# Three drains ahead of the first group's first store in an RMSNorm-and-repeat kernel

## The chip, the cores and the metric

The kernel runs on one core of one Trainium2 chip. The metric is the device time of one execution in microseconds (us). The kernel before the change took 237.68 us, the median of 3 runs (237.47 to 237.84). One further execution was taken under the hardware profiler. It took 236.99 us, of which 235.7 us are the span of the profile, from the first profiled instruction of the program to the last.

## The reference

The input `x` has 8 x 512 = 4096 rows of 2048 float32 values. Each row is divided by its root mean square, multiplied by `gamma`, and written twice, one copy right behind the other. So 33.55 MB are read and 67.11 MB are written.

```python
B, S, D = 8, 512, 2048
x_rep = np.repeat(x, 2, axis=1)
rms = np.sqrt((x_rep ** 2).mean(axis=-1, keepdims=True) + 1e-6)
out = (x_rep / rms) * gamma[None, None, :]      # (8, 1024, 2048) float32
```

## The kernel before

**Tiles.** The 4096 rows are cut into four tiles of 1024 rows, numbered 0 to 3. In a tile each of the 128 partitions holds 8 neighbouring rows, 64 KB. One load (`load`, L50) brings a whole tile, 8.39 MB. A tile gives twice as many output rows, so it is stored in two halves, and each half is again 128 partitions x 64 KB (`store`, L56). There are 4 loads and 8 stores, all of one size, and all are issued by SyncE (SP) on one queue.

**The buffer.** One SBUF tensor `y` of 128 x 24 rows x 2048 holds everything. Its three regions are `first` (rows 0 to 7), `second` (8 to 15) and `third` (16 to 23). One tile of a group is loaded into rows 4 to 11, across `first` and `second`; the other is loaded into `third`.

**The steps.** `squares` (L69, L73, on ScalarE = ACT) makes sums of squares of some rows and their roots. `scale` (L82, L83, on VectorE = DVE) takes the reciprocal and multiplies each row by it and by `gamma`, into every second row of its target region. `repeat` (L90) copies those rows into the gaps between them; some of these copies run on ACT, some on DVE. Then `store` sends the region out.

**The order.** The order of the instructions on each engine is the order of the program (`manual_schedule`, no planner). The function `four` handles two tiles and is called twice, with tiles 0 and 1 (the first group) and with tiles 3 and 2 (the second group, `last=True`). In each call SP does, in this order: two loads, four stores. So its twelve transfers stand in one line: load, load, store x4, load, load, store x4. The loads of the second group go into space that stores of the first group read, so SP waits for those stores to land before it issues them.

**Around the change.** The first store of a group needs two copies: one on ACT and one on DVE. The latter is the return value `copied`. In the second group a helper `behind(copied)` puts 18 drains (`nc.sync.drain()`, L96) on SP ahead of that store. A drain here does nothing but occupy SP's instruction stream, and the first of the 18 waits for the copy on DVE. In the first group there is nothing of the kind: SP comes to the first store early and stands there in three waiting instructions (shown in the profile as EVENT_SEMAPHORE of L56) until the copy is done. These three wait for the five transfers of `gamma` and of tile 0 that have to have landed, and for DVE.

**The end.** After the last store ACT waits for the landing of the last but one store, spends time in three copies (L170), and SP waits for the landing of the last store (L173). This is not touched.

Of the kernel before, what the change touches and what calls it, by code (L numbers as in the profile page):

```python
# [9 lines left out]
def kernel(  # L10
# [38 lines left out]
    def load(n, at):  # L49
        nc.sync.dma_start(out=y[:, at : at + H * K, :], in_=x_t[n])  # L50
# [4 lines left out]
    def store(n, h, to, own=False):  # L55
        dma = nc.sync.dma_start(  # L56
            out=out_t[n, h], in_=y[:, to : to + K * R, :].rearrange("p j d -> p (j d)")
        )
        if own:
            tc.no_tile_sem_insts.add(dma.ins.name)  # L60
            dma.then_inc(landed[h], 16)

    def squares(at, rows):

        n = len(rows)
        ss = small.tile([P, n], f32, name=f"ss{n}")
        for c, k in enumerate(rows):
            sq = junk.tile([P, D], f32, name="sq")
            nc.scalar.activation(  # L69
                out=sq[:], in_=y[:, at + k, :], func=Act.Square, accum_out=ss[:, c : c + 1]  # L70
            )
        rms = small.tile([P, n], f32, name=f"rms{n}")
        nc.scalar.activation(out=rms[:], in_=ss[:], func=Act.Sqrt, scale=inv_d, bias=eps_t[:])  # L73
        return rms

    def scale(at, to, rows, rms, at_once=K):
        n = len(rows)
        rstd = small.tile([P, n], f32, name=f"rstd{n}")
        for c, k in enumerate(rows):
            if c % at_once == 0:  # L80
                part = slice(c, min(c + at_once, n))
                nc.vector.reciprocal(out=rstd[:, part], in_=rms[:, part])  # L82
            nc.vector.scalar_tensor_tensor(  # L83
                out=y[:, to + R * k, :], in0=y[:, at + k, :], scalar=rstd[:, c : c + 1],
                in1=gamma_b[:], op0=Alu.mult, op1=Alu.mult,
            )

    def repeat(to, k0, k1, copy):
        y_r = y[:, to + R * k0 : to + R * k1, :].rearrange("p (k r) d -> p k r d", r=R)
        return copy(out=y_r[:, :, 1, :], in_=y_r[:, :, 0, :]).ins  # L90

    STEPS = 18

    def behind(copied):
        for step in range(STEPS):
            drain = nc.sync.drain().ins  # L96
            if step == 0:
                tc.add_manual_dep(
                    drain, copied.name,
                    mybir.DependencyInfo(mybir.DependencyClass.Sync, mybir.DependencyReason.DATA),  # L100
                    reason="issue time",
                )
# [6 lines left out]
    def four(n, m, constants, at_once, last=False):  # L109


        load(n, first + K)
        constants()
        load(m, third)
        for rows, n_at_once in ((up[:half], half), (up[half:], at_once)):
            scale(first + K, first, rows, squares(first + K, rows), n_at_once)
        repeat(first, 0, half, nc.scalar.copy)
        copied = repeat(first, half, K, nc.vector.tensor_copy)
        if last:
            behind(copied)  # L120
        store(n, 0, first)
        scale(second, second, down, squares(second, down))
        repeat(second, half, K, nc.scalar.copy)
        repeat(second, 0, half, nc.vector.tensor_copy)
        store(n, 1, second)
        roots = [squares(third + h * K, up) for h in range(H)]
        scale(third, first, up, roots[0])
        repeat(first, 0, half, nc.scalar.copy)
        repeat(first, half, K, nc.scalar.copy)
        store(m, 0, first, last)  # L130
        scale(third + K, third, up, roots[1])
        repeat(third, 0, K, nc.scalar.copy)
        store(m, 1, third, last)
# [8 lines left out]
    def constants():  # L142
        nc.gpsimd.memset(eps_t, eps)  # L143

        nc.scalar.activation(out=gamma_s[0:1, 0, :1], in_=eps_t[0:1, :], func=Act.Sqrt)  # L145
        nc.scalar.dma_start(
            out=gamma_s[0:1, :, :C],
            in_=gamma[: G * C].rearrange("(p c d) -> p c d", p=1, c=G),
        )
        for c in range(E):  # L150
            at = G * C + c * G
            nc.scalar.dma_start(
                out=gamma_t[0:1, c * G : (c + 1) * G],
                in_=gamma[at : at + G].partition_broadcast(1),
            )
        nc.gpsimd.partition_broadcast(  # L156
            out_ap=gamma_b[:, : G * C].rearrange("p (c d) -> p c d", c=G),
            in_ap=gamma_s[0:1, :, :C],
        )
        nc.gpsimd.partition_broadcast(out_ap=gamma_b[:, G * C :], in_ap=gamma_t[0:1, : E * G])  # L160

    four(0, 1, constants, 1)
    four(3, 2, lambda: None, half, last=True)

    ctx.close()
# [38 lines left out]
```

## Time and profile before

| what | value |
|---|---|
| time, median of 3 runs | 237.68 us (237.47 to 237.84) |
| profiled execution: time, span | 236.99 us, 235.7 us |
| DVE busy | 84.4 us, 36% of the span |
| ACT busy | 127.6 us, 54% |
| SP's data queue (q1) | 1728 packets, 100.66 MB, 99.0% of 16 DMA engines |
| first store of the first group issued | 39.19 us |
| first store of the second group issued | 156.36 us |

Times are counted from the start of the span. The "share" of a DMA queue is the time that its packets took, summed and divided by 16 engines times the span: 99.0% says that the 16 DMA engines were almost never without a packet of this queue. A packet of the big transfers is one partition's 64 KB. Each transfer has 128 such packets, 8 for each of the 16 engines, so the page's 1728 packets are 12 transfers of 128 data packets and 16 small ones. In a table of windows a packet is counted whole in the window in which it starts; a share above 1 is therefore no error but says that packets that start in the window last beyond it.

### The profile page before, as it was taken

Reading aid. Unit: us, or ns where it says so; the run is one execution under the profiler, and the core shown is the slowest. Engines: PE = TensorE matmul, PEld = TensorE weight load, DVE = VectorE, ACT = ScalarE, POOL = GpSimd, SP = SyncE. Lnnn points to the kernel's source line nnn. Section 1 sums busy time; section 2 is a strip of 40 time slices with the busy share of each in tenths; the row PEclk is TensorE's granted clock in tenths of the full one; section 3 lists DMA queues with packets and bytes.
Section 4 is the critical chain, followed back from the end, with each engine's and each line's share of the span. In section 5 each row is a group of like instructions: output and inputs, shape, how many; then the busy total and the mean of one; then the engine's idle time right before and its main releaser. Section 6 shows DMA issues by size and latency. Waiting matters only on the chain. (4 is left out here: it accounts for less than half of the span.)

```text
span 235.7 us, 251 instructions
## 1 busy us (share of the span) xinstructions
DVE 84.4 (36%) x47; ACT 127.6 (54%) x89; POOL 2.9 (1%) x7
## 2 busy tenths in 40 slices
DVE  0000496594599500000000006938918993000000
ACT  2001989479999370000000049891999966502996
POOL 0110000000000000000000000000000000000000
DMA  9898989989898998989899898989889898989988
GB/s 356 357 534 356 523 367 389 501 356 534 356 523 368 467 423 367 523 356 534 356 456 434 356 534 356 534 356 523 367 389 501 356 534 356 534 356 489 400 356 357
DMA packets 1768, 100.69 MB, mean 427 GB/s; under 512 B 230, under 2 KB 230, under 8 KB 230
## 3 DMA queue, kind: packets, MB, share of 16 engines
q1 hardware_dynamic: 1728, 100.66, 99.0%
q10 hardware_dynamic: 38, 0.01, 0.0%
q14 instruction: 2, 0.02, 0.0%
HBM read 33.56 MB, written 67.11 MB: 427 GB/s over the span
## 5 line engine op out<-in xcount | busy, mean ns | idle before, releaser
L69 ACT ACTIVATE sq<-y 128x2048 f32<-128x2048 f32 x32 | 60.1, 1878 | 72.9 <-DMA y<-in_x_dram 72.2
L83 DVE SCALAR_TENSOR_TENSOR y<-y,rstd,gamma_b 128x2048 f32<-128x2048 f32 x32 | 73.8, 2348 | 1.8 <-DMA out_dram<-y 1.2
L90 ACT COPY y<-y 128x4096 f32<-128x4096 f32 (+1 forms) x10 | 42.6, 4283 | 19.2 <-DVE y L83 18.5
L82 DVE RECIPROCAL rstd<-rms 128x4 f32<-128x4 f32 (+2 forms) x11 | 1.8, 168 | 109.9 <-ACT rms L73 109.9
L170 ACT COPY y<-y 1x8192 f32<-1x8192 f32 (+1 forms) x3 | 17.4, 5876 | 13.0 <-ACTq L168 13.0
L90 DVE COPY y<-y 128x4096 f32<-128x4096 f32 x4 | 9.2, 2293 | 0.1
L69 ACT ACTIVATION_READ_ACCUMULATOR sq<-y 128x1 f32 x32 | 6.0, 186 | 0.0
L73 ACT ACTIVATE rms<-ss,eps_t 128x4 f32<-128x4 f32 (+1 forms) x10 | 3.0, 296 | 0.3
L156 POOL PARTITION_BROADCAST gamma_b<-y x1 | 2.2, 2245 | 9.8 <-DMA y<-in_gamma_dram 9.8
L145 ACT ACT_TABLE_LOAD x1 | 1.3, 1283 | 0.7 <-PEq L188 0.7
L160 POOL PARTITION_BROADCAST gamma_b<-y x1 | 0.3, 323 | 10.0 <-DMA y<-in_gamma_dram 10.0
L145 ACT ACTIVATE y<-eps_t 1x1 f32<-1x1 f32 x1 | 0.2, 202 | 0.0
L143 POOL MEMSET eps_t<- 128x1 f32 x1 | 0.1, 100 | 0.3 <-POOLq L188 0.3
L188 POOL MEMSET const-uint8-127<- 128x1 uint8 x1 | 0.1, 103 | 0.0
L188 POOL MEMSET const-float32-0.0<- 128x1 f32 x1 | 0.1, 99 | 0.2 <-issue 0.2
L188 POOL MEMSET const-bfloat16-1.0<- 128x1 bf16 x1 | 0.1, 101 | 0.0
L188 POOL MEMSET const-float32-1.0<- 128x1 f32 x1 | 0.1, 98 | 0.0
## 6 DMA issues: line engine op xcount, KB each, us to landing
out_dram<-y SPq DMA_DIRECT2D x8, 24.9
y<-in_x_dram SPq DMA_DIRECT2D x4, 31.4
y<-in_gamma_dram ACTq DMA_DIRECT2D x3, 0.1 KB
y<-in_gamma_dram ACTq DMA_DIRECT2D x1, 7.8 KB, 8.2
```

Of the source, the lines that this page charges most:

```text
L69: nc.scalar.activation(out=sq[:], in_=y[:, at + k, :], func=Act.Square, accum_out=ss[:, c : c + 1])
L73: nc.scalar.activation(out=rms[:], in_=ss[:], func=Act.Sqrt, scale=inv_d, bias=eps_t[:])
L82: nc.vector.reciprocal(out=rstd[:, part], in_=rms[:, part])
L83: nc.vector.scalar_tensor_tensor(out=y[:, to + R * k, :], in0=y[:, at + k, :], scalar=rstd[:, c : c + 1], in1=gamma_b[:], op0=Alu.mult, op ...
L90: return copy(out=y_r[:, :, 1, :], in_=y_r[:, :, 0, :]).ins
L143: nc.gpsimd.memset(eps_t, eps)
L145: nc.scalar.activation(out=gamma_s[0:1, 0, :1], in_=eps_t[0:1, :], func=Act.Sqrt)
L156: nc.gpsimd.partition_broadcast(out_ap=gamma_b[:, : G * C].rearrange("p (c d) -> p c d", c=G), in_ap=gamma_s[0:1, :, :C],)
L160: nc.gpsimd.partition_broadcast(out_ap=gamma_b[:, G * C :], in_ap=gamma_t[0:1, : E * G])
L170: done = nc.scalar.copy(out=y[0:1, a:b, :], in_=y[0:1, a:b, :])
L188: nc = _bacc.Bacc("TRN2", target_bir_lowering=False, num_devices=1)
```

## The change

`behind` takes the number of drains as an argument. It is now called in both groups: with 18 in the second, as before, and with 3 in the first. The first of the three drains waits for the DVE copy `copied`; the first store stands behind the third. In the built program SP's instructions ahead of that store are then, in order: drain (waits for DVE), drain, drain, the same three waiting instructions as before, the store. Nothing else is moved on any engine.

```diff
-    STEPS = 18
-
-    def behind(copied):
-        for step in range(STEPS):
+    def behind(copied, steps):
+        for step in range(steps):
             drain = nc.sync.drain().ins
             if step == 0:
                 tc.add_manual_dep(
...
         copied = repeat(first, half, K, nc.vector.tensor_copy)
-        if last:
-            behind(copied)
+        behind(copied, 18 if last else 3)
         store(n, 0, first)
```

## The prediction

> **What bounds the kernel now.** I read the page's busy times, its DMA queues and its chain first. DVE is busy for 36% of the span and ACT for 54%, while the queue that SP issues on fills 99.0% of the time of all 16 DMA engines. The chain of work that ended last names only the copies of L170, 7% of the span, which run beside the last store.
>
> ```profile
> span 235.7 us, 251 instructions
> ...
> DVE 84.4 (36%) x47; ACT 127.6 (54%) x89; POOL 2.9 (1%) x7
> ...
> q1 hardware_dynamic: 1728, 100.66, 99.0%
> ...
> ACT y L170 7%
> ```
>
> So the span is a line of packets. Each DMA engine carries 12 transfers x 8 packets = 96 packets of 64 KB. What one packet takes is read from the table of windows: in 154.90 to 155.50 us 1748 GB/s x 0.60 us = 1.049 MB started, 16 packets, and the share 4.03 x 0.60 us gives 2.418 us each. 96 x 2.418 = 232.1 us. The trace's records of single packets have the first packet at 1.73 us and the end of the last at 235.16 us, 233.4 us apart. All that is lost between the two is 1.3 us, and 0.9 of it is the very first row of packets (one took up to 3.30 us). Only two things can change the time: an engine that runs dry, or a packet that lasts longer than 2.418 us.
>
> The second view is the timeline around the two first stores, as lines of start, duration, engine, line and operation.
>
> ```profile
> 36.82 2.29 DVE L90 COPY y<-y 128x4096 f32<-128x4096 f32 x1
> ...
> 39.19 0.35 SPq L56 DMA_DIRECT2D out_dram<-y  x1
> ```
>
> ```profile
> 153.04 2.29 DVE L90 COPY y<-y 128x4096 f32<-128x4096 f32 x1
> ...
> 156.36 0.34 SPq L56 DMA_DIRECT2D out_dram<-y  x1
> ```
>
> In the first group the copy ends at 39.11 and the store is issued 0.08 us later. In the second it ends at 155.33 and the store comes 1.03 us later. What lies between them there is 18 drains and one waiting instruction.
>
> ```profile
> L96 SPq DRAIN  x18: 7/7/7, 155.4 to 156.2; - x18
> ```
>
> The third view is the table of windows (length, DVE, ACT, POOL, clock, DMA share, GB/s) around the seam between a group's second load and its first store, first group and then second.
>
> ```profile
> 38.60:39.20 0.60, 0.51 (x1) 0.60 (x1) 0.00 (x0) 1.00 4.08 1748
> 39.20:41.10 1.90, 0.00 (x0) 1.87 (x3) 0.00 (x0) 1.00 0.00 0
> ...
> 154.90:155.50 0.60, 0.43 (x1) 0.60 (x1) 0.00 (x0) 1.00 4.03 1748
> 155.50:157.30 1.80, 0.00 (x0) 1.77 (x3) 0.00 (x0) 1.00 0.00 0
> 157.30:157.90 0.60, 0.00 (x0) 0.57 (x3) 0.00 (x0) 1.00 4.05 1748
> ```
>
> The last row of 16 packets of the load starts in 38.60 to 39.20. No packet starts until 41.10, as every engine has one in hand; then the store's packets follow on. In the packet records the first engine to be free is so at 41.13 and the last at 41.76, and each goes on with the store in under 0.02 us. The reader is to see that the store was issued 41.13 - 39.19 = 1.94 us before anyone needed it.
>
> **The change part by part.** *The drains.* They delay nothing but SP. By the records of SP's instructions in the second group the drains stand 0.052 us apart (first at 155.363, last at 156.241, 17 steps), the waiting instruction follows 0.058 us behind the last, and the store 0.058 us behind that. Where SP has waiting instructions in a row (203.758, 203.820, 203.884, 203.946) they stand 0.063 us apart.
>
> *The three waiting instructions.* Before, SP had gone through two of them by 22.8 us and stood in the third, so they cost nothing after the copy. Now the first drain takes that wait, and all three come after it. Sum from the first drain (0.03 us behind the copy, as in the second group: 39.14): 2 x 0.052 + 0.058 + 2 x 0.063 + 0.058 = 0.35, so the store is issued at 39.49 and not 39.19. The delay is 0.30 us, twice what three drains alone are (0.16).
>
> *What it costs on the path.* The cover is the last row of the load, until 41.13. From 39.49 there are 1.64 us left. What a store needs from issue to its first packet the trace bounds but doesn't show: at the start of the program the first load was issued at 0.72 and its first packet began at 1.73, 1.01 us; in the second group the store was issued at 156.36, the first engine was free at 157.34, 0.98 us later, and went on at once. So 1.01 us is an upper bound from a cold queue and 0.98 from a running one. Both are under 1.64. I cost the delay at nothing; if the cover were gone, the whole 0.30 us would show.
>
> *Behind the store on SP* stand the waits of the second store, issued at 55.80, and of the third at 76.07; both wait for copies that end later than any of this. Nobody waits for this store's issue but DVE at L83, which waits 0.7 us for its landing (61.1), and the loads of the second group, issued at 100.10 and needed at 118.7. No DMA is added, none changes its place in the line, and no other engine's instructions move.
>
> *What it could gain.* The last row of the load differs in the two groups: 4.08 x 0.60 = 2.448 us a packet in the first, with the store issued 0.06 to 0.48 us after those packets started, and 4.03 x 0.60 = 2.418 in the second, issued 0.89 to 1.44 us after. That is 0.030 us x 16 = 0.48 us of lengthening in the first. By the packet records 0.215 of it falls on the engine that starts last and ends last (39.13 to 41.76), 0.10 and 0.08 on two others. With the change the store is issued 0.36 to 0.79 us after the starts, between the two cases. The gain is between 0 (the lengthening stays, or it is made up later: in the row that starts at 115.9 to 116.5 the other engines lose 0.1 to 0.44 us while this one loses 0.05) and 0.215 us (it goes, and nothing eats it). Whether the issue causes the lengthening no row tells. I take 0.08, nearer the low end, since by 118.7 us another engine is the last to finish and the lead of the others is spent.
>
> *Sum.* Span 235.66 - 0.08 + 0.00 = 235.58; the profiled execution 236.99 would be 236.91. The median of the runs shown lies 0.69 above the profiled one, and I leave that as it is: 237.68 - 0.08 = 237.6 us. A difference of 0.2%, 0.48 us, is about what a measurement of this kernel can tell from no change (its three runs lie 0.37 us apart).
>
> **A rule weighed here.** The row is the 0.98 us of the second group, with no idle DMA engine at the seam. The Trainium skill, page "DMA: Bandwidth & Descriptors", section "Rules for kernel authors", advises to issue a DMA early, because a fixed setup cost then overlaps with other work; its section on the anatomy of one DMA puts that fixed cost at about 2.0 us for the GpSimd path. Taken whole as a delay ahead of the first packet, that would be an estimate by that page of the Trainium skill of 39.49 + 2.0 = 41.49, a gap of 0.36 us at the seam, where the row gives none. By the same reckoning the second group's seam would have a gap of 1.0 us, and the trace shows none there, so I go by the row.
>
> **The rivals.** *The engines run dry at the seam (slower, but little).* If a store in the first group needed more than 1.64 us from issue to first packet, every engine would wait. For: the latency is not shown for this place. Against: 0.98 us sufficed at 156.36. A seam without idle time before caps the need at 1.94 us, so the gap is at most 1.94 - 1.64 = 0.30 us: 237.98 us, still within 0.2%.
>
> *The lengthening grows (slower).* The issue falls into the middle of the in-flight packets' first half and lengthens the last row more than now. For: rows exist that are far longer, 0.44 us at 116.0 where the line goes from store to load, and 0.88 us in the first row of all. Against: the later issue of the second group had none. With 0.88 on the engine that ends last in place of 0.215 the time is 237.68 + 0.67 = 238.35; with 0.44 it is 237.9. It decides from 0.69 us (0.215 + 0.48) on.
>
> *The lengthening goes, and more than one engine's share with it (faster).* If all 0.48 us of the row are carried one after another by the engine that sets the end, or the unprofiled runs, which are 0.69 us longer than the profiled one, lose more at this seam than the profiled one, the time is 237.68 - 0.48 = 237.2 or less. For: the second group with its later issue has a clean seam. Against: the records show 0.215 at most on one engine, and 0.30 us is only a third of the second group's delay.
>
> *It does nothing at all*, the last row is lengthened as before: 237.68, which the forecast cannot be told from.
>
> **How the numbers follow.** Forecast, with the case of no effect: 0.70. Running dry, up to 0.30 us: 0.06; both lie within 0.2%, so "same" has 0.76. Lengthening gone in a larger measure, over 0.48 us: 0.14, faster. Lengthening grown beyond 0.69 us: 0.10, slower. The range reaches from the faster rival's 237.2 to the dry seam's 237.98 and a little beyond, 238.05; it leaves out part of the two outer cases.
>
> **What would show it.** In the changed kernel's trace three drains of L94 stand at about 39.14 to 39.24, the first store is issued at 39.49 (39.34 if the three waiting instructions don't count), and the second group's store still 1.03 us behind its copy. In the windows the last row of load two starts in 38.6 to 39.2, the store's row from 41.1 on, and nothing lies idle between; the share of the first window tells whether the lengthening went (4.03) or stayed (4.08) or grew. The prediction is wrong if the store's first row starts later than 41.13 plus the longest packet, or if the queue's 99.0% falls, or if the time moves by more than 0.48 us while the seam looks the same.

## The result and the profile after

The changed kernel takes 238.40 us, the median of 20 runs, against 237.05 us for the kernel before, also of 20 runs. The first three of them are the runs with the median of 237.68 us that the prediction starts from; they lay high. The ratio is 1.0042, with a 95% interval of 1.0028 to 1.0056: 1.3 us slower, outside the range that was forecast.

The runs themselves say more than the median. Of the 20 runs of the changed kernel four lie at 236.9 to 237.0 us, where the kernel before has its fastest runs (from 236.84 on), and sixteen lie between 237.9 and 239.0 us. Of the kernel before only one run of the 20 was above 238.0 us, and 2 of 141 over all sessions. So the change does not add a constant to every execution. It makes a long kind of execution common that was rare. The profiled execution of the changed kernel (238.39 us, span 237.1 us) is of the long kind.

The page of the changed kernel, its queue and the row of the sums of squares (busy, mean, idle before and what ended it), and then the same row of the kernel before:

```profile
span 237.1 us, 254 instructions
...
q1 hardware_dynamic: 1728, 100.66, 98.6%
...
L69 ACT ACTIVATE sq<-y 128x2048 f32<-128x2048 f32 x32 | 60.1, 1878 | 74.5 <-DMA y<-in_x_dram 73.8
```

```profile
L69 ACT ACTIVATE sq<-y 128x2048 f32<-128x2048 f32 x32 | 60.1, 1878 | 72.9 <-DMA y<-in_x_dram 72.2
```

The queue's share fell from 99.0 to 98.6%, and ACT waits 1.6 us longer for tiles to land (73.8 us, before 72.2). The first store's copy and issue in the timeline of the changed kernel:

```profile
36.97 2.29 DVE L90 COPY y<-y 128x4096 f32<-128x4096 f32 x1
...
39.65 0.35 SPq L56 DMA_DIRECT2D out_dram<-y  x1
```

The copy ends at 39.26 and the store comes 0.39 us behind it; before it was 0.08. That is the change as it was meant, and nothing is late yet. The delay shows 100 us further on, where the second group begins. First the kernel before, then the changed one:

```profile
138.95 1.88 ACT L69 ACTIVATE sq<-y 128x2048 f32<-128x2048 f32 x1 [51.79 <-DMA y<-in_x_dram]
...
156.36 47.30 SPq L56 DMA_DIRECT2D out_dram<-y  x4
```

```profile
140.41 1.88 ACT L69 ACTIVATE sq<-y 128x2048 f32<-128x2048 f32 x1 [53.31 <-DMA y<-in_x_dram]
...
157.82 0.34 SPq L56 DMA_DIRECT2D out_dram<-y  x1
```

Tile 3 is there 1.46 us later, and the second group's first store is issued 1.46 us later. The loss has arisen by 140 us. The table of windows shows where. The first window holds the last row of 16 packets of the second load, the second the last row of the fourth store, the third the first row of tile 3's load. First before, then after (length, DVE, ACT, POOL, clock, DMA share, GB/s):

```profile
38.40:39.40 1.00, 0.71 (x1) 1.00 (x2) 0.00 (x0) 1.00 2.45 1049
115.80:117.30 1.50, 0.00 (x0) 0.00 (x0) 0.00 (x0) 1.00 1.73 699
118.30:120.60 2.30, 0.00 (x0) 0.00 (x0) 0.00 (x0) 1.00 1.06 456
```

```profile
38.40:39.40 1.00, 0.86 (x1) 1.00 (x1) 0.00 (x0) 1.00 2.43 1049
115.80:117.30 1.50, 0.00 (x0) 0.00 (x0) 0.00 (x0) 1.00 1.84 699
118.30:120.60 2.30, 0.00 (x0) 0.00 (x0) 0.00 (x0) 1.00 1.10 456
```

Each window holds 16 packets (GB/s times length is 1.049 MB), so share times length is the mean of one. The row at 38.4 became shorter, 2.43 us in place of 2.45. The row at 115.8 became longer: 2.60 us before (1.73 x 1.5), 2.76 after, where an undisturbed packet takes 2.418. So did the row at 118.3, 2.44 before and 2.53 after. A mean of 0.16 and 0.09 us hides that most of it falls on few engines: by the packet records one store packet takes 1.02 us more than 2.418, and one load packet 1.17 us more. They are on different engines, since the load packet starts at 119.58 and the store packet ends at 119.71. The last engine lands tile 3 at 140.06 us (before 138.56).

From there the loss runs on to the end. In the changed kernel no engine starts a data packet between 157.4 and 158.6, since the store was only issued at 157.82:

```profile
157.40:158.60 1.20, 0.00 (x0) 1.20 (x1) 0.00 (x0) 1.00 0.01 0
158.60:158.90 0.30, 0.00 (x0) 0.30 (x1) 0.00 (x0) 1.00 7.68 3277
```

The last packet ends at 236.71, before at 235.16.

What happened at the first store itself is small. In the packet records 15 of the 16 engines go from the load on to the store within 0.01 us. One is free at 41.20 and starts its first store packet at 41.39: 0.19 us of idle time on one engine. This engine begins with the store 1.74 us after its issue (39.651 to 41.388). Whether this engine is one of those that lose 78 us later can't be told: the records do not name a packet's engine, and on the way there packets of different engines start within a few ns of each other.

### The profile page after: what moved, and what is told of

Same layout as the page of the kernel before. It is cut to its first block, busy times and chain, and to the rows that moved or that the text cites. A ratio compares the mean times of both kernels' runs of the same rounds, so it can differ in the third digit from the quotient of the medians.

```text
span 237.1 us, 254 instructions
## 1 busy us (share of the span) xinstructions
DVE 84.4 (36%) x47; ACT 127.6 (54%) x89; POOL 2.9 (1%) x7
## 3 DMA queue, kind: packets, MB, share of 16 engines
q1 hardware_dynamic: 1728, 100.66, 98.6%
## 5 line engine op out<-in xcount | busy, mean ns | idle before, releaser
L69 ACT ACTIVATE sq<-y 128x2048 f32<-128x2048 f32 x32 | 60.1, 1878 | 74.5 <-DMA y<-in_x_dram 73.8
L83 DVE SCALAR_TENSOR_TENSOR y<-y,rstd,gamma_b 128x2048 f32<-128x2048 f32 x32 | 73.8, 2348 | 1.6 <-DMA out_dram<-y 1.0
```

Source lines behind the costliest of these rows:

```text
L69: nc.scalar.activation(out=sq[:], in_=y[:, at + k, :], func=Act.Square, accum_out=ss[:, c : c + 1])
L83: nc.vector.scalar_tensor_tensor(out=y[:, to + R * k, :], in0=y[:, at + k, :], scalar=rstd[:, c : c + 1], in1=gamma_b[:], op0=Alu.mult, op ...
```

## The experiments

Two theories stood at the beginning. **A**: the later issue of the first store is the cause, through what it does to the DMA engines. **B**: it is the drains or the three more instructions on SP. In what follows a *seam* is the passage of the 16 engines from one transfer to the next. The *lead* of a transfer is the time from its issue to the first engine that comes free. The *excess* of a row is what its 16 packets take above 2.418 us each, summed over the engines. Idle times and excesses of single rows are from the packet records of the one profiled execution of each kernel; "long" counts runs above 238.0 us. The figure called before is the kernel before, run again beside each group of experiments.

**The drains without the delay.** `e1_drains_early` is the kernel before with three drains right behind the first two loads.

```diff
         load(m, third)
+        if not last:
+            for _ in range(3):
+                nc.sync.drain()
```

> The kernel before, with the three drains put on SyncE right behind the first two loads, where they run at about 2 us and delay no store: the first store is issued at 39.2 us as before. Theory A (the later issue of the first store is the cause, through what it does to the DMA engines at later seams): no change, 237.05 us like before, ratio 1.000. Theory B (three more instructions in SyncE's stream are the cause, wherever they stand): 238.4 us, ratio 1.004 or more.

Measured: 237.17 us, before 237.09, ratio 1.0006 (0.9992 to 1.0019); 0 of 12 runs long. Theory B in its first form, more instructions in SP's stream, is out.

**The delay without the drains.** `e2_copy_late` puts two tiny reciprocals ahead of the copy on DVE.

```diff
+        if not last:
+            for _ in range(2):
+                nc.vector.reciprocal(out=late[:], in_=eps_t[:])
         copied = repeat(first, half, K, nc.vector.tensor_copy)
...
+    late = singles.tile([P, 1], f32, name="late")
```

> The kernel before without any drain in the first group, but with two tiny reciprocals (128x1 into a scratch tile, an addition to the work) on VectorE ahead of the copy that the first store waits for: the copy ends some 0.35 us later, the store is issued at about 39.55 us, SyncE's instructions are those of before. Theory A (issue time): slower like the changed kernel, about 238.4 us, ratio 1.004. Theory B (SyncE's instructions): 237.05 us, ratio 1.000.

Measured: 237.56 us, ratio 1.0016 (1.0006 to 1.0026), and no run long, but also none below 237.25. It reached only part of its aim: the copy began at 37.06 us, 0.24 us later than before, and 0.09 of that was there before the reciprocals. The lead was 1.58 us and no engine ran dry. The 0.4 us that all runs have more come from elsewhere. The packet records show a fetch of instructions, 8 KB, at 210.63 us, which takes 0.31 us on one of the 16 DMA engines in the middle of the last stores, and in the end one engine finishes 0.46 us behind all others (235.44, the next at 234.98). In the kernel before that fetch comes at 235.32, behind the last data packet. Two instructions more on DVE brought it forward.

`f3_copy_later` does it again with one longer copy and with two reciprocals merged, so that DVE has as many instructions as before.

```diff
+        if not last:
+            nc.vector.tensor_copy(out=late[:], in_=gamma_b[:, :700])
         copied = repeat(first, half, K, nc.vector.tensor_copy)
...
+    late = singles.tile([P, 700], f32, name="late")
...
-    four(0, 1, constants, 1)
+    four(0, 1, constants, half)
```

> The kernel before with no drain in the first group; in its place one copy of 128x700 elements into a scratch tile (an addition to the work) on VectorE ahead of the copy that the first store waits for, and the two last reciprocals of that stage made in one, so that VectorE has as many instructions as before. The store is issued about 0.3 to 0.4 us later than before, at 39.5 to 39.6 us, by VectorE alone. Theory A (issue time): executions near 238.5 us appear in half or more of the runs and the median is above 238 us. Theory B (drains or waits on SyncE itself): no execution above 238 us, median 237.05 to 237.2 us. If an instruction fetch of 8 KB falls among the last stores, as it did at 210.6 us with two instructions more, every execution is 0.4 us longer.

In its timeline:

```profile
36.82 0.52 DVE L119 COPY late<-gamma_b 128x700 f32<-128x700 f32 x1
37.25 2.29 DVE L90 COPY y<-y 128x4096 f32<-128x4096 f32 x1
...
39.61 0.35 SPq L56 DMA_DIRECT2D out_dram<-y  x1
```

Measured: 237.13 us, before 236.90, ratio 1.0018 (1.0003 to 1.0034), 3 of 12 runs long, the highest 238.88. The profiled execution is one of the long ones (238.82): two engines idle at the first store, 0.36 us in sum, which begin 1.80 and 1.82 us after the issue, tile 3 landed at 140.27, the second group's first store issued at 158.05. So the delay alone, with no drain in the first group, makes the long executions. Their share is lower than expected (a half or more), so A holds in kind and the dose decides how often.

**The dose.** `f1_one_drain`, `f2_eight_drains` and `f4_fourteen_drains` change only the number of drains in the first group.

```diff
-        behind(copied, 18 if last else 3)
+        behind(copied, 18 if last else 1)      # 8, 14
```

> One drain in place of three: the store is issued 0.20 us later than before in place of 0.30 (the three waiting instructions behind the drain cost as much as with three). Theory A (issue time): with 0.08 us of delay no execution was above 238 us and with 0.30 us 16 of 20 were, so 0.20 gives some share of such executions between, and a median of 237.2 to 238.3 us. Theory B: the same 238.4 us as with three, as the wait already stands on a drain.

> Eight drains in place of three: issue 0.56 us later than before, near 39.8 us, still 1.3 us ahead of the first free engine at 41.1. Theory A (issue time, by a clean last row of the second load): the last row is already clean with three, so the same slow executions, median 238 to 238.5 us. If instead each 0.05 us of delay adds to the loss, it grows with the count: 239 us or more.

> Fourteen drains: issue 0.87 us later than before, near 40.1 us, 1.0 us ahead of the first free engine, which is where the second group's store stands in the kernel before without harm. If only the place of the issue against the last row mattered, as in the second group, no loss: 237.05 us. If the later seam from stores to loads at 116 to 119 us is where the first group pays, which the second group does not have, the slow executions stay: 238 to 238.5 us.

Measured, with before at 236.90: one drain 237.07 us (ratio 1.0017, 1.0004 to 1.0030), 3 of 12 long; eight 238.51 (1.0068, 1.0056 to 1.0080), 5 of 5 long; fourteen 238.91 (1.0082, 1.0069 to 1.0095), 4 of 4 long. In the windows of the kernel with fourteen drains:

```profile
38.40:39.40 1.00, 0.75 (x1) 1.00 (x2) 0.00 (x0) 1.00 2.42 1049
115.80:117.30 1.50, 0.00 (x0) 0.00 (x0) 0.00 (x0) 1.00 2.02 699
118.30:120.60 2.30, 0.00 (x0) 0.00 (x0) 0.00 (x0) 1.00 1.19 456
```

The last row of the load is now quite undisturbed (2.42 us), and the row at 115.8 takes 3.03 us a packet (2.02 x 1.5) against 2.60 before: 0.43 us more on the mean engine, for an idle time at the first store of 0.17 us an engine. The second group's store, whose lead is also 1.0 us, does no harm before; the first group's does. Neither expectation for eight drains held whole. Among the long runs alone three drains and eight have the same median, 238.51 us. Over all runs the loss against before is 1.35, 1.61 and 2.01 us with three, eight and fourteen drains, 0.05 to 0.07 us for each drain more, where a drain delays the issue by 0.052 us.

**The second group's drains.** `e3_three_and_none` is the changed kernel without the 18 drains of the second group, `g4_none_none` the kernel before without them.

```diff
-        behind(copied, 18 if last else 3)
+        if not last:
+            behind(copied, 3)              # g4: no call at all
```

> The changed kernel without the 18 drains of the second group. If the loss is that tile 3 lands 1.5 us late on one DMA engine and the first store of the second group, held 0.94 us more by its 18 drains, then comes too late for the engines (they ran dry from 157.43 to 158.67 us), the store is issued 0.94 us earlier and most of the dry time goes: 237.5 us, ratio 1.002. If the loss has nothing to do with that seam: 238.4 us or more.

> The kernel before without its 18 drains in the second group, no drain anywhere: the second group's first store is issued 0.95 us earlier, near 155.4 us. If the 18 drains leave that seam with no room, so that every lateness of tile 3 turns into dry time, executions above 237.2 us become rarer and the median is 236.85 to 237.0 us. If they do good by keeping the last row of the second load clean, it loses up to 0.2 us: 237.2 us.

Measured: `e3` 237.93 us, before 237.09, ratio 1.0032 (1.0012 to 1.0051), 6 of 12 long, and these 6 at 238.45 to 238.98, no shorter than the long runs of the changed kernel. `g4` 237.15, before 237.06, ratio 1.0001 (0.9990 to 1.0013). Neither expectation of a gain held. The profile of `e3` (a long execution, 238.45) says why. Its second group's store is issued at 156.92, the engines hardly run dry (0.05 us each), and still the last packet ends at 236.75.

```profile
156.92 0.34 SPq L56 DMA_DIRECT2D out_dram<-y  x1
```

The few engines that are up to 1.9 us late carry that to the end by themselves, and the idle time that the 18 drains give the others costs nothing on top. My reading of the profile after, that the gap at 157.4 to 158.6 is the loss, was wrong: the gap is only how the other engines wait for the late ones.

**The second load.** `e4_load_late` holds back the second group's second load, whose issue at 120.1 us lay inside the packet that took 1.17 us more.

```diff
+    sent = []
...
+        sent.append(dma.ins)
...
+        if last:
+            behind(sent[-1], 30)           # waits for the last store of the first group
         load(m, third)
```

> The changed kernel with 30 drains (1.55 us) ahead of the second load of the second group, behind the same landing that this load waits for: it is issued at about 121.5 us in place of 120.1, still 16 us ahead of need. If the issue of that load is what lengthened the in-flight packet of tile 3 by 1.17 us (119.58 to 123.17 us), that lengthening goes and the time falls to about 237.3 us. If the switch of the engines from stores to loads at 116 to 119 us is the cause, nothing changes: 238.4 us.

Measured: 237.63 us, ratio 1.0046 (1.0024 to 1.0068), 5 of 12 long, up to 239.72. The issue went to 121.15 us and the long executions stayed. By itself this does not clear the issue, as 121.15 would still lie inside a packet like that of the changed kernel (119.58 to 123.17). The order of time in the changed kernel says more: of the 7.4 us of excess from the last row of stores to the second row of loads, 5.5 lie on the row of stores, and its last packet ended at 119.71, ahead of this issue at 120.10. So the issue does not start the loss; that it has a part in the long load packet is not ruled out. The short ones lie at 237.44 to 237.63, again 0.5 us up: the queue for instructions has one fetch more, at 208.50 us, from the 30 instructions added to SP.

```profile
q14 instruction: 3, 0.02, 0.0%
```

**The other direction.** `g3_split_copy` issues the first store earlier, by splitting the last copy between ACT and DVE.

```diff
-        copied = repeat(first, half, K, nc.vector.tensor_copy)
+        if last:
+            copied = repeat(first, half, K, nc.vector.tensor_copy)
+        else:
+            repeat(first, half, half + 1, nc.scalar.copy)
+            repeat(first, half + 1, K, nc.vector.tensor_copy)
```

> The opposite of the change: the kernel before with the copy of the first group's last two rows split, one row on ScalarE and one on VectorE, so that the first store is issued about 1.1 us earlier, near 38.1 us, 3 us ahead of the first free engine. Theory C (what counts is that no engine runs dry at this seam): no execution above 238 us, median 236.85 to 237.1 us like before, at its floor. If an issue near the last row's start is what disturbs that row and sets up the later seam, it is slower or faster than before by 0.2 us or more.

Measured: 237.72 us, before 237.06, ratio 1.0025 (1.0017 to 1.0034). All 11 runs lie between 237.5 and 238.1, so this is a cost of every execution. Its timeline and windows:

```profile
36.89 1.23 DVE L90 COPY y<-y 128x2048 f32<-128x2048 f32 x1
...
38.19 0.35 SPq L56 DMA_DIRECT2D out_dram<-y  x1
```

```profile
38.40:39.40 1.00, 0.00 (x0) 0.97 (x3) 0.00 (x0) 1.00 3.21 1049
```

With a lead of 3.7 us the packets of the load's last row take 0.79 us more on the mean (3.21 against 2.42; the least 0.58, the most 1.18). The lead contains this lengthening: the first engine is free at 41.91, where it was 41.13 before. So "no engine runs dry" is not all; the theory that the kernel before is at its floor there fell, and the issue time has a window with two edges. The Trainium skill, page "DMA: Bandwidth & Descriptors", section "Rules for kernel authors", advises to issue a DMA early. At this seam that differs from the measurement: 1.0 us earlier cost 0.66 us.

**Is the first store slow because it is the first?** `g2_small_store` sends a 16x128 store ahead of it, with fourteen drains.

```diff
+        if not last:
+            nc.sync.dma_start(out=warm_d, in_=warm_s[0:16, :])
         load(m, third)
...
```

> Fourteen drains in the first group as in the run at 238.9 us, and in addition a small store of 16x128 elements to a scratch tensor in HBM between the first two loads (an addition to the work, 16 packets). With fourteen drains alone the engines were fed 1.17 to 1.70 us after the issue of the first store and 13 of 16 ran dry, while the second group's first store feeds them in 0.85 to 0.99 us. Theory E (the first store of the program is slow to feed the engines because it is the first): fed within 1.0 us, hardly an engine dry, 237.2 us. Theory F (the place or the time, not being the first): still 1.2 to 1.7 us, dry, 238.5 to 239.2 us.

Measured: 239.09 us, before 237.06, ratio 1.0075 (1.0060 to 1.0090), 6 of 6 long; idle time at the first store 3.0 us over the engines. The earlier store changed nothing, so being the first store is not the reason.

**Running dry elsewhere.** `g1_thirty_last` makes the second group's first store late, with no loads behind it; `h3_second_late` makes the first group's second store late, with the loads still to come.

```diff
-    STEPS = 18
+    STEPS = 30
```

> The kernel before with 30 drains in place of 18 in the second group and none in the first: its first store is issued 0.62 us later, near 157.0 us, so that by the 0.85 to 0.99 us that this seam needs from issue to packet the engines run dry for 0.3 to 0.5 us. No loads follow this seam. Theory C (a dry seam costs little itself; it costs in the first group because the later seam from stores to loads multiplies it): the loss is the dry time alone, 237.3 to 237.6 us, in nearly all runs alike. Theory D (a dry seam costs 1 to 2 us wherever it is): 238.4 us or more.

```diff
-        repeat(second, half, K, nc.scalar.copy)
-        repeat(second, 0, half, nc.vector.tensor_copy)
+        if last:
+            repeat(second, half, K, nc.scalar.copy)
+            repeat(second, 0, half, nc.vector.tensor_copy)
+        else:
+            repeat(second, 0, K, nc.scalar.copy)
```

> The kernel before, no drain in the first group, with the first group's second store made late instead: all four rows of its copy on ScalarE, so that it is issued near 60.5 us, just as the engines come free at 60.4 us, and all of them run dry for about 0.85 us. Theory J (running dry at any seam ahead of the loads makes the seam at 116 to 120 us cost more): 239 us or more, that seam's excess far above 3.5 us over the engines. Theory K (only the seam from loads to stores does that): the dry time alone, about 237.9 us, and the later seam as before.

`g1`: 237.26 us, before 237.06, ratio 1.0008 (0.9999 to 1.0018), 0 of 11 long. Its windows show the gap, 14 of 16 engines idle for 0.16 to 0.8 us, 7.8 us in sum:

```profile
157.30:157.90 0.60, 0.00 (x0) 0.60 (x2) 0.00 (x0) 1.00 0.01 0
```

Idle time of 0.49 us on the mean engine cost 0.2 us, less than itself, because the engine that ends last was not among the idle ones. `h3`: 242.85 us, ratio 1.0247 (1.0234 to 1.0260). It overshot, as ACT's longer copy made the third store late too: the engines were idle 0.6 us at 61 and 4.2 us at 81 to 85 us. In its windows one row of packets starts in the 7 us from 79 on, where nearly three would fit:

```profile
79.00:86.00 7.00, 6.96 (x4) 5.06 (x2) 0.00 (x0) 1.00 0.35 151
```

These 4.8 us leave 1.0 of the 5.8 us unaccounted for. The excess at the later seam, from 121.3 us here, was 13.1 us over the engines (before 3.5), though at the first store itself no engine ran dry. So it is not a property of that one store: by these two runs, running dry ahead of the passage from stores to loads goes with a dearer passage, and behind it it does not matter beyond its own length. It is not in proportion to the idle time: 4.8 us on every engine, 77 in sum, brought 9.6 us of excess, and 2.2 in sum brought 9.2 in `f2`.

**Does the later seam hang on the lead of the load?** `h1_late_load` and `h2_late_load_drains` (with fourteen drains) were to hold tile 3's load back to 116.8 us.

```diff
+        if last:
+            for a, b in ((0, 8192), (0, 8192), (0, 3072)):
+                spare = y[0:1, second + K : third, :].rearrange("p k d -> p (k d)")[:, a:b]
+                paused = nc.scalar.copy(out=spare, in_=spare)
+            behind(paused.ins, 1)
         load(n, first + K)
...
```

> The kernel before (no drain in the first group) with the first load of the second group held back to about 116.8 us by three copies on ScalarE of rows that are free by then (an addition to the work, off the path), 1.9 us ahead of the first free engine at 118.7 in place of 18.6 us. At the first store's seam a lead of 3.7 us lengthened the last row by 0.8 us an engine and leads of 1.6 to 1.9 us by 0.01 to 0.03 us. Theory G (the seam from stores to loads behaves alike: its 0.2 us an engine come from the load being queued long before): the lengthening of the row at 116 us falls below 0.1 us an engine, the runs above 237.2 us go, median 236.6 to 236.9 us. Theory H (the seam's cost comes from the direction of the switch, whatever the lead): 237.05 us as before; or, if loads need more lead than stores, slower by the dry time.

> The same late load with 14 drains ahead of the first store, the case that took 238.9 us. Theory G: what the dry first seam hands on to the seam at 116 to 120 us (15 us over the engines in place of 3.5) is paid only because the load is queued early; with a lead of 1.9 us it goes, 237.1 us or a little more for the dry time of 0.17 us an engine. Theory H: 238.5 us or more, as with 14 drains alone.

These two are inconclusive: ACT began the copies at 87.0 us, when store two had long landed, and the load went out at 104.0 (lead 14.6 us). `h1` 236.99 us, ratio 1.0003 (0.9991 to 1.0015); `h2` 239.24, ratio 1.0086 (1.0068 to 1.0105). Longer copies, 1x16384 twice and 1x1700, put it right in `h4_lead_two` and `h5_lead_two_drains`; the edit is otherwise the same.

> The kernel before with the first load of the second group held back to about 116.75 us, as meant in the run before, which held it to 104.0 us only (ScalarE's copies started at 87.0 us and not at 100). Two copies of 1x16384 and one of 1x1700 elements on ScalarE are added to the work, off the path; the lead over the first free engine at 118.7 is 1.9 us. Theory G (that seam's lengthening comes from the load being queued long before): the excess of the row at 116 us falls from 2.8 us over the engines to below 1.5, the runs above 237.2 us go, median 236.6 to 236.9 us. Theory H (the lead does not matter): 237.0 us and a tail as before; or slower by dry time, if this seam needs more than 1.9 us.

> The same lead of 1.9 us with 14 drains ahead of the first store (238.9 us with the early load). Theory G: what the dry first seam hands on is no longer paid at the seam at 116 to 120 us: 237.1 to 237.4 us. Theory H: 238.5 us or more.

`h4`: 238.13 us, before 237.03, ratio 1.0033 (1.0014 to 1.0052), 7 of 12 long. `h5`: 238.33, ratio 1.0051 (1.0034 to 1.0067), 6 of 6 long. The load was issued at 116.45 (lead 1.9 us), and in the windows of `h4`:

```profile
115.80:117.30 1.50, 0.00 (x0) 0.45 (x1) 0.00 (x0) 1.00 1.61 699
118.30:120.60 2.30, 0.00 (x0) 0.00 (x0) 0.00 (x0) 1.00 1.16 456
```

The stores' last row is undisturbed (1.61 x 1.5 = 2.42 us), and now the load's first row pays, 2.67 us a packet against 2.44. The passage's price moved from one side of the seam to the other, and the long executions became more. Theory G, that it would go, fell.

**The profiles by the first store's lead.** One profiled execution each, ordered by lead; sums over the 16 engines in us. The later seam is the excess of the last row of stores and the first two rows of loads.

| kernel | lead | excess, load's last row | idle at the first store | excess, later seam | runs long |
|---|---|---|---|---|---|
| `g3` | 3.72 | 12.7 | 0 | 1.7 | 1 of 11 |
| before | 1.94 | 0.50 | 0 | 3.5 | 2 of 141 |
| `e1` | 1.92 | 0.34 | 0 | 3.5 | 0 of 12 |
| `g4` | 1.71 | 0.44 | 0 | 4.6 | 0 of 12 |
| `f1` | 1.61 | 0.28 | 0 | 4.3 | 3 of 12 |
| `e2` | 1.58 | 0.15 | 0 | 3.9 | 0 of 12 |
| `e4` | 1.57 | 0.19 | 0 | 3.8 | 5 of 12 |
| `f3` | 1.50 | 0.14 | 0.4 | 7.1 | 3 of 12 |
| after | 1.39 | 0.15 | 0.2 | 7.4 | 15 of 20 |
| `e3` | 1.17 | 0.11 | 0.9 | 10.2 | 6 of 12 |
| `f2` | 1.15 | 0.07 | 2.2 | 12.7 | 5 of 5 |
| `f4` | 0.94 | 0.04 | 2.7 | 15.4 | 4 of 4 |
| `g2` | 0.69 | 0.00 | 3.0 | 17.0 | 6 of 6 |

(The profiled executions of `e4` and `f1` are short ones, with a lead at the edge.) Two more fit in: `g1` (lead 1.81 us, no idle time, excess at the later seam 4.1) and `h1` (1.67, none, 4.2). `h2` (0.65, idle 3.1, excess 13.0) and `h5` (0.87, 2.5, 10.2), whose load was held back as well, lie lower than their idle time would put them; `h3` and `h4` change a seam in between. The idle time begins between 1.57 and 1.50 us of lead, and in the same place the later seam jumps from about 4 to 7 and then grows with the idle time, by four times as much or more. Above the edge nothing jumps until, at 3.7 us, the load's last row pays 12.7; between 1.94 and 3.7 us the table has no row.

## Why the prediction was wrong

**The delay** was right. The first drain was forecast at 39.14 and stood at 39.29, because the copy ended 0.15 us later; from the drain to the store 0.35 us were forecast and 0.36 measured (39.288 to 39.651), the three waiting instructions included. No DMA was added and no other engine's order changed.

**The lengthening of the load's last row** was right in kind. It went with the later issue, from 0.50 us over the engines to 0.15, and with one, eight and fourteen drains it is 0.28, 0.07 and 0.04. Without a delay it scatters (0.31 in `g1`, 0.90 in `h4`, 1.60 in `h3`). The gain of 0.08 us that I took from it can't be seen beside the rest.

**The cover** is the step that failed: "I cost the delay at nothing", with 1.01 us as an upper bound for what a store needs. Both rows under that bound were of other places, a load into an empty queue and the second group's store. At this seam the engine that ran dry began 1.74 us after the issue, and two in `f3` 1.80 and 1.82 us, and engines already run dry at a lead of 1.50 us. The true cover before was not 1.94 - 1.01 but 1.94 - 1.5, about 0.4 us. In the profiled execution the lead fell by 0.55 us, to 1.39: about 0.31 by the change, 0.15 by a copy that ended later and 0.09 by a first engine that was free earlier. That went through it. The remark that the latency "is not shown for this place" was the warning; it got a rival with a chance of 0.06.

**The price of running dry** failed as well. The sentence "if the cover were gone, the whole 0.30 us would show" and the rival's cap of 0.30 us take the idle time as its own price. It was 0.19 us on one engine, and the executions became 1 to 2 us longer. The price arises at the passage from stores to loads 75 us later, which the forecast named only as a place where others lose a lead. That is why the case that I put down as "slower, but within 0.2%" gave the largest change.

**Nobody waits** for this issue, said the forecast, but DVE and the loads with 18 us to spare. By semaphores that is so. The link is not a semaphore; it lies in the packets of the DMA engines, by a mechanism that stays open.

**The other rival on the slow side**, a longer last row from an issue at a worse point, does exist, but for an earlier issue (`g3`, 0.79 us an engine) and not for a later one. That the 0.88 us of the very first row came near this size is luck, as it was taken from another place.

**The rule weighed in the forecast**, to issue a DMA early (the Trainium skill, page "DMA: Bandwidth & Descriptors", section "Rules for kernel authors"), pointed the right way for this change. I set it aside for the second group's 0.98 us, which was a row of another seam. By `g3` it fails in the other direction.

**Smaller readings.** The 0.69 us by which the runs lay above the profiled execution was the luck of three runs: over 20 runs the median is 237.05, 0.06 above it. The landing of the first store given as 61.1 us is 61.46, and the row said to start at 115.9 to 116.5 starts at 115.99 to 116.63. That another engine is the last to finish by 118.7 us, which set the 0.08, can't be read from records that do not name the engines.

What stays open: by what mechanism idle time at one seam raises the excess of another. That the later issue raises it is shown by `f3` (delay alone), `e1` (drains alone) and the number of drains. That idle time is the link is argued from the order in the table, with one profile of each kernel, and from `h3` against `g1` (dry ahead of the passage, dry behind it). It is not that the engines have fallen out of step: the packets ahead of the stores' last row end within 0.64 us of each other before, 0.59 in the changed kernel and 0.17 in `h3`. Which engine pays is not known. Nor is it known why this seam needs 1.5 us of lead.

## What to carry to other kernels

In a kernel whose DMA engines are never idle, the lead of each transfer over the first free engine is a quantity to be read from the packets at every seam, and a bound from another seam need not hold; here, in the profiled executions, 1.6 to 1.9 us was good, 1.5 too little and 3.7 too much. Idle time of engines in the middle of a run is not priced by its length: what comes behind it, here a passage from stores to loads, can bring a loss several times as long (in the changed kernel 0.2 us on one engine went with 1.5 us at the end), and one late engine of sixteen is enough to delay the whole tile. Look at all runs, not at the median alone: here two heaps of times meant that something was at its edge, and the size of a small delay decided how often it went over.

## What the hardware showed unexpectedly

- The second group's first store, issued late, fed its first idle engine after nearly the same time in four profiles: 0.846 us after the issue in the changed kernel (157.820 to 158.666), 0.849 in `g1`, 0.841 in `f4`, 0.843 in `g2`. Where all 16 engines were idle, in `h3` at 61 and at 85 us, all were fed within 0.83 to 0.99 us. It is no constant of that seam: in `h3` five idle engines at the second group's first store began 1.39 to 1.52 us after the issue. At the first group's store idle engines started between 41.1 and 42.0 us whether the issue was at 39.61 (`f3`) or at 40.36 (`g2`).
- A transfer queued 3.7 us ahead lengthens the last packets of the one before by 0.79 us each where the direction changes from load to store; queued 1.6 to 2.0 us ahead, by 0.01 to 0.10 (0.03 in the kernel before, 0.10 in `h3`).
- An instruction fetch is one 8 KB packet that takes 0.31 us on one of the 16 DMA engines. Two instructions more on DVE moved one from behind the last store to 210.6 us, and the fastest execution became 0.4 us longer (237.25 against 236.84). The Trainium skill, page "Runtime: NRT & Kernel Launch", section "Instruction fetch mechanics", calls the cost of a block boundary mostly hidden; where all DMA engines are busy to the end, the measurement differs. In this kernel an experiment that adds instructions must be looked at for that first.
